# Weight sums from GpSimd to VectorE, half-piece reloads of token sums, and the final norm's weights, in a decoder layer on one core

## The chip, the cores and the metric

The kernel runs on one core of a Trainium2 chip. The metric is the time of one execution on the device in microseconds (us). The engines are TensorE (PE; its weight loads are PEld), VectorE (DVE), ScalarE (ACT), GpSimd (POOL) and SyncE (SP), which here only issues DMA transfers. Each engine takes its instructions strictly in the order of its own queue.

## The reference

One layer of a hybrid decoder, for 2048 tokens of width 1024 in float32: two kinds of attention side by side, then a feed-forward part with squared ReLU, then a norm. The part that matters here:

```python
h = h + jnp.einsum('bsm,md->bsd', mixed, w_out[l])
nm = rmsnorm(h, mlp_norm_g[l])
a = jnp.square(jax.nn.relu(jnp.einsum('bsd,df->bsf', nm, w_ff1[l])))   # 1024 -> 4096
h = h + jnp.einsum('bsf,fd->bsd', a, w_ff2[l])                         # 4096 -> 1024
return rmsnorm(h, final_norm_g)
```

## The kernel before

A float32 product is made as three matmuls of rounded parts: an operand is split into a high part (ScalarE copies with rounding) and a low part (VectorE subtracts), and `mm3` issues high × high, low × high and high × low. The products are also done by fast matrix schemes, which need fewer block products but sums of blocks beforehand.

**First feed-forward product.** The tokens are cut in two halves of 1024; each half is worked as 7 block products for each of 16 groups of columns, so 2 × 16 × 7 = 224 jobs (`jobs1`), each of 12 matmuls (`product1`). The seven sums of token blocks that a half needs were written to memory earlier (`hTD`), and are read back into a buffer `rb` and split into `TF` (tiles named `hb`) before the half's first job. There are two `rb` buffers of 128 × 2048. `reload(j, half)` starts the load of a whole sum, 1024 KB, and returns a generator whose two steps split half of it each. From job `first` = 105 on, where the last group of the first half begins, `parts_at` spreads the 14 half splits over the jobs 106 to 116; the second half's first job is 112. While `product1` runs, `act_sums` makes sums of the activations and writes them to `actD`.

**Second feed-forward product.** It is worked as 26 phases (`PRODUCTS`), each one block product of activations (`ca`, from `actD` by way of `ra`) and weights (`cb`). A phase has four steps, one for each quarter of the inner dimension; a step has 2 × 4 × 3 = 24 matmuls. The weights' operand of a step lies in one of four quarters of a state (`bs`), and the next phase's is made from it: where the table says `=`, `update_b` loads the state anew; where it says `+` or `-`, it adds a block that `fetch_b` has loaded into one of four buffers `rb` (in the profile these have the same name as the token buffers). `prep_b` then splits the state into one of three buffers `cb`, `prep_a` an activation block into one of three `ca`. In `update_b` the first sum of a step goes to GpSimd and a second one to VectorE (`engines=(G, V)`); only the four steps before the stage starts have both on VectorE. 88 sums are made: 22 of the table's entries, four steps each.

A new load of a state may start when VectorE has split the old one; a sum on it follows the load. `taken` adds a phase's result from PSUM to the running sums `acc2`, and where an output block is complete, `output` makes the final norm: two squares with a row sum on ScalarE, the factor `r`, one half of the row multiplied by `r` and the norm's weights on VectorE (line 1520), the other by the weights on GpSimd (1517) and by `r` on ScalarE (1521).

**Order.** The program is written as one sequence, and `tc` is made with `schedule_with_timeline_sim=True`: when the program is built, a planner runs it on a model of the engines and fixes each engine's queue in the order in which the instructions become ready there. So an instruction can stand in a queue ahead of others that were written before it.

```python
            update_b(n + 4)
            if n + 6 not in fetched:
                fetch_b(n + 6)
            prep_a(n + 2)
            prep_b(n + 2)
```

Of the kernel before, what the change touches and what calls it, by code (L numbers as in the profile page):

```python
# [13 lines left out]
AF = mybir.ActivationFunctionType  # L14
OP = mybir.AluOpType
# [101 lines left out]
def emit(tc, a, stop=99):  # L117
    nc = tc.nc
    V, A, G, T, SP = nc.vector, nc.scalar, nc.gpsimd, nc.tensor, nc.sync
# [6 lines left out]
    def ps(tag):  # L126
        return psum.tile([128, 512], F32, name="ps_" + tag, tag=tag, bufs=BANKS[tag])

    def slot(name, dt=F32, n=SLOT):

        return up.tile([128, SLOT], dt, name=name, tag="u", bufs=25)[:, :n]
# [34 lines left out]
    def stat(n=1):  # L166
        if stat_at[0] + n > 48:
            stat_at[0] = 0
        s = stats[:, stat_at[0]:stat_at[0] + n]
        stat_at[0] += n  # L170
        return s

    def rstd_of(ssq, width, n=1, bias=eps):
        r = stat(n)
        A.activation(r, ssq, AF.Ln, bias=bias, scale=1.0 / width)
        A.activation(r, r, AF.Exp, scale=-0.5)
        return r
# [46 lines left out]
    hTD = dram.tile([2, 7, 128, 4, 512], F32, name="hTD")  # L224
# [15 lines left out]
    CX, c11, c12, c21, c22, last = [t[:, GP * q:GP * q + GP] for t in acc for q in range(2)]  # L240
# [11 lines left out]
    order = (1, 2, 5, 6, 3, 4, 7)  # L252
# [4 lines left out]
    TF = {j: [slot(f"tb{j}", FR) for _ in range(2 if j < 7 else 1)] for j in order}  # L257
# [227 lines left out]
    def split(hi, lo, src):  # L485
        A.activation(hi, src, AF.Copy)  # L486
        V.tensor_tensor(lo, src, hi.bitcast(F32), op=OP.subtract)  # L487
# [109 lines left out]
    def reload(n):  # L597

        j, cs = order[n // 2], slice(1024 * (n % 2), 1024 * (n % 2) + 1024)
        t = (xp, bp)[n // 2 % 2][:, cs]  # L600
        SP.dma_start(t, nTD[j - 1].rearrange("p c s -> p (c s)")[:, cs])

        def rest():
            hi, lo = [v[:, cs] for v in TF[j]]
            tc.keep_in_program_order(A.activation(hi, t, AF.Copy))
            V.tensor_tensor(lo, t, hi.bitcast(F32), op=OP.subtract)
            if n + 4 < 14:
                back.append(reload(n + 4))

        return rest  # L610
# [121 lines left out]
    for at in range(7, len(jobs)):  # L732
        g = jobs[at][0]
# [419 lines left out]
    for pr in range(4):  # L1153
# [3 lines left out]
        for hh, br in seq:  # L1157
# [3 lines left out]
            first = len(units)  # L1161
# [62 lines left out]
    rb, TF, TB = [slot("rb")], {}, {}  # L1224
# [53 lines left out]
    order = (1, 2, 6, 5, 7, 3, 4)  # L1278
# [10 lines left out]
    def prep1(at):  # L1289

        if at >= len(jobs1):
            return
        g, j = jobs1[at]
        if not combs1:
            combs1.extend(view(c[:, 1024 * q:], (2, 4, 128)) for c in [slot("w1comb", FR) for _ in range(2)]
                          for q in range(2))
        r = raw1[g % 2]
        (a11, a12), (a21, a22) = [[r[:, 4 * k:4 * k + 4, n * 128:n * 128 + 128] for k in range(2)] for n in range(2)]
        c = combs1[at % 4]
        split(c[:, 0], c[:, 1], {1: a11, 2: a12, 6: a11, 5: a21, 7: a11, 3: a12, 4: a22}[j])  # L1300
        if j == 1:
            V.tensor_tensor(a21, a21, a22, op=OP.add)
            V.tensor_tensor(a11, a21, a11, op=OP.subtract)
        if j == 2:
            V.tensor_tensor(a12, a12, a11, op=OP.subtract)
        if j == 6:
            V.tensor_tensor(a11, a22, a11, op=OP.subtract)
        if j == 4:
            load_w1(g + 2)
# [80 lines left out]
    def some_sums(n=3):  # L1390

        for _ in range(n):
            while sums1 and next(sums1[0], 0) == 0:
                sums1.pop(0)
# [5 lines left out]
    for at, t in enumerate(tiles):  # L1400
# [8 lines left out]
        p = [ps("a"), ps("a")]  # L1409
        parts_ = 2 if at < 2 else 1  # L1410
        for q in range(parts_):
            for n in range(2):
                cs = slice(n * 512, n * 512 + 512)
# [20 lines left out]
    raw_a, comb_a, raw_b, comb_b, state, fin = [], [], [], [], [], {}  # L1434
# [5 lines left out]
    def load_a(n):  # L1440

        if n < 2 * NPH:
            p, k = divmod(n, 2)
            if len(raw_a) < 2:
                raw_a.append(view(slot("ra"), (4, 512)))
            SP.dma_start(raw_a[n % 2], actD[AT[p], :, 4 * k:4 * k + 4].rearrange("p q h s -> p q (h s)"))

    def prep_a(n):

        if n >= LAST:  # L1450
            return
        if len(comb_a) < 3:
            comb_a.append(view(slot("ca", FR), (2, 2, 512)))
        c, r = comb_a[n % 3], raw_a[n // 2 % 2][:, n % 2 * 2:n % 2 * 2 + 2]
        if PRODUCTS[n // 4][0] > 0:
            split(c[:, 0], c[:, 1], r)
        else:
            A.activation(c[:, 0], r, AF.Copy, scale=-1.0)
            V.scalar_tensor_tensor(c[:, 1], r, -1.0, c[:, 0].bitcast(F32), op0=OP.mult, op1=OP.subtract)
        if n % 2:  # L1460
            load_a(n // 2 + 2)
# [3 lines left out]
    def w2_part(n, k, m):  # L1465

        first = 8 * (n % 4) + 2 * (k % 2) + k // 2
        return w2[:, first:first + 5:4, 512 * m:512 * m + 512]

    def state_of(n):  # L1470

        if len(state) < 2:
            state.extend(view(slot("bs"), (4, 512)) for _ in range(2))
        return state[n % 4 // 2][:, n % 2 * 2:n % 2 * 2 + 2]

    def fetch_b(n):

        if n >= LAST:
            return
        if not raw_b:  # L1480
            raw_b.extend(view(v[:, 1024 * e:], (2, 512)) for v in [slot("rb2") for _ in range(2)] for e in range(2))
        fetched[n] = []
        for op, k, m in PRODUCTS[n // 4][2]:
            if op != "=":
                v = raw_b[turns[0] % 4]
                turns[0] += 1
                SP.dma_start(v, w2_part(n, k, m))
                fetched[n].append((op, v))

    def update_b(n, engines=(G, V)):  # L1490

        if n >= LAST:
            return
        v = state_of(n)
        for op, k, m in PRODUCTS[n // 4][2]:
            if op == "=":
                SP.dma_start(v, w2_part(n, k, m))
        for e, (op, r) in enumerate(fetched.pop(n)):
            engines[e].tensor_tensor(v, v, r, op=OP.add if op == "+" else OP.subtract)  # L1499

    def prep_b(n):

        if n >= LAST:
            return
        if len(comb_b) < 3:
            comb_b.append(view(slot("cb", FR), (2, 2, 512)))
        v = comb_b[n % 3]
        split(v[:, 0], v[:, 1], state_of(n))

    def output(C, row, i, last=False):  # L1510

        scr = fin["scr"][:, 512 * (i % 2):512 * (i % 2) + 512]
        ss, part = stat(2), stat()
        for n in range(2):
            A.activation(scr, C[n], AF.Square, accum_out=ss[:, n:n + 1])
            if n == 0:
                G.tensor_tensor(C[0], C[0], fin["g"][:, :512], op=OP.mult)
                A.activation(part, ss[:, 0:1], AF.Copy, bias=EPS, scale=1.0 / D)
        r = rstd_of(ss[:, 1:2], D, bias=part)
        V.scalar_tensor_tensor(C[1], C[1], r, fin["g"][:, 512:], op0=OP.mult, op1=OP.mult)  # L1520
        A.activation(C[0], C[0], AF.Copy, scale=r)
        SP.dma_start(out2[row:row + 128, 512:], C[1])
        (A if last else SP).dma_start(out2[row:row + 128, :512], C[0])

# [58 lines left out]

    first, parts_at = 7 * (NP - 1), {}
    for n in range(14):
        parts_at.setdefault(first + 1 + n * 4 // 5, []).append(n // 2)
    halves, begun = {}, set()
    for at in range(7, len(jobs1)):
        if at == first - 2:
            halves.update({n: reload(order[n], 1) for n in range(2)})  # L1590
        prep1(at + 2)
        some_sums()
        product1(at)
        for n in parts_at.get(at, ()):
            next(halves[n])
            if n in begun and n + 2 < 7:
                halves[n + 2] = reload(order[n + 2], 1)
            begun.add(n)
        n = at + 6 - len(jobs1)
        if n == 0:  # L1600
            load_a(0)
        if 0 <= n < 4:
            fetch_b(n)
            update_b(n, (V, V))
        if n == 3:
            load_a(1)
        if n in (3, 5):
            prep_b(n // 2 - 1)
            prep_a(n // 2 - 1)
            fetch_b(n // 2 + 3)  # L1610
# [4 lines left out]
    for ph, (_, chained, _, _) in enumerate(PRODUCTS):  # L1615
# [3 lines left out]
        for k in range(4):  # L1619
            n = 4 * ph + k  # L1620
# [74 lines left out]
```

## Time and profile before

| | us |
|---|---|
| median of 3 runs | 2280.32 (2277.76 to 2281.45) |
| the profiled execution | 2283.21 |
| its span, from the first to the last instruction | 2281.4 |
| PE busy | 2249.2 |
| VectorE busy | 1630.4 |
| ScalarE busy | 1230.4 |
| GpSimd busy | 544.3 |

In a row of the profile stand the line of the program, the engine, the operation, the tiles written and read, the shapes, the count, the busy time with the mean of one instruction in ns, and the idle time of the engine before these instructions with what ended it. A matmul counts as busy until its modelled end, so two neighbours overlap; how fast TensorE goes is seen from the starts. The granted clock is the share of TensorE's full speed. An "SPq" row is the issue of a transfer by SP; the transfer lands some us later.

### The profile page before, as it was taken

How to read it: one execution, taken by the hardware profiler on the slowest of the kernel's cores; microseconds unless marked ns; L12 is line 12 of the kernel's file. 1: busy time of each engine (PE TensorE's matmuls, PEld its weight loads, DVE VectorE, ACT ScalarE, POOL GpSimd, SP SyncE). 2: the span in 40 equal slices, each digit the busy share in tenths (PEclk: the TensorE clock that was granted, in tenths of full speed). 3: DMA queues.
4: the chain of work that ended last, by engine and by line, in shares of the span. 5: the costliest groups of instructions: out<-in, count | busy, mean ns of one | idle time of the engine just before them, and what ended most of it. 6: DMA issues, size and time to landing. Idle time of an engine off the chain costs nothing.

```text
span 2281.4 us, 35136 instructions
## 1 busy us (share of the span) xinstructions
PE 2249.2 (99%) x12508; PEld 1945.9 (85%) x12508; DVE 1630.4 (71%) x3065; ACT 1230.4 (54%) x2436; POOL 544.3 (24%) x482
## 2 busy tenths in 40 slices
PE   9999999999999999999999999999999999999998
PEld 8978998899999998888888887888888878888876
DVE  8788878766667676446777778777777577576778
ACT  6665436426877874234555556555555433333446
POOL 1210002024385672000000000000007562032465
PEclk9999999999999999999999999999999999999999
DMA  5458754776768864678544456555479988676775
GB/s 201 134 182 245 252 155 136 223 234 221 223 196 255 262 207 139 221 232 273 185 138 153 137 161 202 163 165 163 128 266 285 311 279 277 214 254 227 261 255 175
DMA packets 359920, 478.59 MB, mean 210 GB/s; under 512 B 19333, under 2 KB 268694, under 8 KB 347712
## 3 DMA queue, kind: packets, MB, share of 16 engines
q1 hardware_dynamic: 355246, 467.69, 63.6%
q0 software_dynamic: 4352, 8.39, 2.0%
q8 instruction: 98, 1.61, 0.3%
q14 instruction: 78, 0.64, 0.1%
q10 hardware_dynamic: 146, 0.27, 0.0%
HBM read 326.54 MB, written 154.44 MB: 211 GB/s over the span
## 4 chain that ended last, share of the span: by engine, by line
PE 84%; DMA 5%; POOL 3%; DVE 3%; issue 3%; ACT 2%; SPq 0%; POOLq 0%; ACTq 0%; DVEq 0%
PE ps_a L143 9%; PE ps_a L142 9%; PE ps_a L144 9%; PE ps_c L143 7%; PE ps_c L142 7%; PE ps_c L144 7%; PE ps_a L893 4%; PE ps_o L142 3%; PE ps_o L144 3%; PE ps_o L143 3%; PE ps_d L143 3%; PE ps_d L142 3%; PE ps_d L144 3%; PE ps_d L874 3%; PE ps_c L852 2%
## 5 line engine op out<-in xcount | busy, mean ns | idle before, releaser
L1499 POOL TENSOR_TENSOR bs<-bs,rb 128x1024 f32<-128x1024 f32 x72 | 217.7, 3031 | 1072.3 <-DMA actD<-ring 836.9
L486 ACT ACTIVATE cb<-bs 128x1024 fp32r<-128x1024 f32 x104 | 110.2, 1060 | 272.7 <-issue 116.2
L487 DVE TENSOR_TENSOR cb<-bs,cb 128x1024 fp32r<-128x1024 f32 x104 | 165.2, 1589 | 124.4 <-ACT cb L486 123.7
L487 DVE TENSOR_TENSOR w1comb<-w1raw,w1comb 128x512 fp32r<-128x512 f32 x224 | 153.8, 689 | 96.4 <-ACT w1comb L486 95.5
L486 ACT ACTIVATE w1comb<-w1raw 128x512 fp32r<-128x512 f32 x224 | 140.3, 628 | 81.6 <-PE ps_c L144 29.5
L865 ACT ACTIVATE pe<-pe,O 128x256 f32<-128x256 f32 (+1 forms) x384 | 156.5, 453 | 45.8 <-DVE O L864 42.3
L893 PE MATMUL ps_a<-v,pt 128*128 128x65 f32 x1200 | 178.5, 253 | 2.5 <-ACT pt L881 1.9
L893 PEld LDWEIGHTS ps_a<-v,pt 128*128 128x128 f32 x1200 | 175.4, 196 | 3.5 <-ACT pt L881 2.1
L874 PE MATMUL ps_d<-ident,pe 128*128 128x128 f32 x600 | 159.7, 279 | 0.0
L864 DVE CUSTOM_DVE_ANT_0 pe<-ps_c,nb 128x256 f32<-128x256 f32 (+1 forms) x384 | 126.3, 361 | 40.9 <-PE ps_d L874 18.3
L286 ACT ACTIVATE wcomb<-wraw 128x512 fp32r<-128x512 f32 (+2 forms) x119 | 90.0, 757 | 98.8 <-PE ps_a L143 34.5
L142 PE MATMUL ps_c<-hb,w1comb 128*128 128x512 f32 x336 | 131.0, 390 | 0.5 <-ACT xs L1371 0.5
L143 PE MATMUL ps_c<-hb,w1comb 128*128 128x512 f32 x336 | 130.9, 390 | 0.0
L144 PE MATMUL ps_c<-hb,w1comb 128*128 128x512 f32 x336 | 130.2, 390 | 0.0
L487 DVE TENSOR_TENSOR ca<-ra,ca 128x1024 fp32r<-128x1024 f32 x84 | 126.8, 1511 | 3.8 <-ACT ca L486 3.8
L142 PE MATMUL ps_c<-cb,ca 128*128 128x512 f32 x312 | 122.1, 391 | 0.0
L143 PE MATMUL ps_c<-cb,ca 128*128 128x512 f32 x312 | 122.0, 391 | 0.0
L144 PE MATMUL ps_c<-cb,ca 128*128 128x512 f32 x312 | 122.0, 391 | 0.0
L351 POOL TENSOR_TENSOR acc<-acc,misc 128x264 f32<-128x264 f32 (+1 forms) x32 | 38.7, 1221 | 313.1 <-DMA wraw<-w_in 200.3
L874 PEld LDWEIGHTS ps_d<-ident,pe 128*128 128x128 f32 x600 | 110.0, 187 | 0.1
L142 PE MATMUL ps_a<-wo,mT 128*128 128x512 f32 x256 | 101.4, 396 | 0.0
L1362 ACT ACTIVATE acc<-acc 128x512 f32<-128x512 f32 x96 | 60.7, 632 | 74.1 <-DVE acc L1381 44.0
(410 smaller groups left out, 7146.7 us busy)
## 6 DMA issues: line engine op xcount, KB each, us to landing
ra<-actD SPq DMA_DIRECT2D x52, 1024.0 KB, 7.3
actD<-ring SPq DMA_DIRECT2D x176, 256.0 KB, 2.5
rb<-w_ff SPq DMA_DIRECT2D x88, 512.0 KB, 6.1
bs<-w_ff SPq DMA_DIRECT2D x72, 512.0 KB, 6.1
w1raw<-w_ff SPq DMA_DIRECT2D x32, 1024.0 KB, 5.7
k<-kD SPq DMA_DIRECT2D x16, 1024.0 KB, 7.4
rb<-hTD SPq DMA_DIRECT2D x13, 1024.0 KB, 5.9
wraw<-w_in SPq DMA_DIRECT2D x48, 256.0 KB, 3.9
```

The costliest lines, as they stand in the source:

```text
L142: T.matmul(out, sh, mh, start=first, stop=False, **kw)
L143: T.matmul(out, sl, mh, start=False, stop=False, **kw)
L144: T.matmul(out, sh, ml, start=False, stop=last, **kw)
L286: A.activation(hi, src, AF.Copy, scale=sc)
L486: A.activation(hi, src, AF.Copy)
L487: V.tensor_tensor(lo, src, hi.bitcast(F32), op=OP.subtract)
L864: V.tensor_tensor_reduce(p, s, bias, scale=1.0, scalar=BIG, op0=OP.add, op1=OP.min, accum_out=nm)
L865: A.activation(p, p, AF.Exp, bias=nm, scale=-1.0)
L874: T.transpose(pb[:, i * 128:i * 128 + 128], src, ident)
L893: T.matmul(self.b.opsum[:, n % 4], self.pt[:, i * 128:i * 128 + 128], self.b.v[:, blk, cols], start=first, stop=last)
L1362: A.activation(v, v, AF.Relu)
L1499: engines[e].tensor_tensor(v, v, r, op=OP.add if op == "+" else OP.subtract)
```

## The change

Three edits. The sums of `update_b` are all made on VectorE. In `output`, the half that GpSimd and ScalarE worked on is multiplied by `r` and the weights in one instruction on VectorE, except for the very last output, which stays as it was. And the token sums of the second half are loaded in 14 pieces of 512 KB: four half buffers hold a piece each, the first four loads are issued at job 102 in place of two whole loads at job 103, and the load of piece n + 4 is issued behind the split of piece n. The jobs at which the pieces are split stay the same.

```diff
-    def update_b(n, engines=(G, V)):
+    def update_b(n, engines=(V, V)):
...
         for n in range(2):
             A.activation(scr, C[n], AF.Square, accum_out=ss[:, n:n + 1])
             if n == 0:
-                G.tensor_tensor(C[0], C[0], fin["g"][:, :512], op=OP.mult)
+                if last:
+                    G.tensor_tensor(C[0], C[0], fin["g"][:, :512], op=OP.mult)
                 A.activation(part, ss[:, 0:1], AF.Copy, bias=EPS, scale=1.0 / D)
         r = rstd_of(ss[:, 1:2], D, bias=part)
         V.scalar_tensor_tensor(C[1], C[1], r, fin["g"][:, 512:], op0=OP.mult, op1=OP.mult)
-        A.activation(C[0], C[0], AF.Copy, scale=r)
+        if last:
+            A.activation(C[0], C[0], AF.Copy, scale=r)
+        else:
+            V.scalar_tensor_tensor(C[0], C[0], r, fin["g"][:, :512], op0=OP.mult, op1=OP.mult)
...
     for n in range(14):
-        parts_at.setdefault(first + 1 + n * 4 // 5, []).append(n // 2)
-    halves, begun = {}, set()
+        parts_at.setdefault(first + 1 + n * 4 // 5, []).append(n)
+    piece = lambda n: rb[n // 2 % 2][:, 1024 * (n % 2):1024 * (n % 2) + 1024]
+
+    def load_piece(n):
+
+        if n < 14:
+            SP.dma_start(piece(n), hTD[1, order[n // 2] - 1][:, 2 * (n % 2):2 * (n % 2) + 2].rearrange("p c s -> p (c s)"))
+
     for at in range(7, len(jobs1)):
-        if at == first - 2:
-            halves.update({n: reload(order[n], 1) for n in range(2)})
+        if at == first - 3:
+            for n in range(4):
+                load_piece(n)
         prep1(at + 2)
         some_sums()
         product1(at)
         for n in parts_at.get(at, ()):
-            next(halves[n])
-            if n in begun and n + 2 < 7:
-                halves[n + 2] = reload(order[n + 2], 1)
-            begun.add(n)
+            cs = slice(1024 * (n % 2), 1024 * (n % 2) + 1024)
+            split(*[v[:, cs] for v in TF[order[n // 2]]], piece(n))
+            load_piece(n + 4)
```

## The prediction

> **What bounds the kernel now.** I read the page's engine rows first, then busy time by stretches, then the groups of matmuls with idle time.
>
> ```profile
> PE 2249.2 (99%) x12508; PEld 1945.9 (85%) x12508; DVE 1630.4 (71%) x3065; ACT 1230.4 (54%) x2436; POOL 544.3 (24%) x482
> ```
>
> The next rows are stretches: length, busy time of PE, PEld, DVE, ACT and POOL, granted clock, DMA share, GB/s.
>
> ```profile
> 1357.00:1402.00 45.00, 39.73 (x160) 31.89 (x159) 38.39 (x60) 31.59 (x49) 0.00 (x0) 0.92 0.63 205
> 1825.00:1875.00 50.00, 47.93 (x203) 37.06 (x202) 36.59 (x34) 16.63 (x17) 29.75 (x12) 1.00 0.89 282
> 1875.00:2160.00 285.00, 285.00 (x1259) 236.11 (x1258) 193.45 (x171) 107.77 (x116) 79.69 (x32) 1.00 0.75 250
> 2160.00:2190.00 30.00, 25.74 (x102) 20.73 (x101) 29.35 (x18) 15.45 (x31) 26.88 (x11) 0.89 0.73 249
> 2190.00:2262.00 72.00, 70.53 (x311) 58.08 (x310) 59.29 (x47) 38.96 (x83) 44.38 (x18) 1.00 0.58 192
> ```
>
> PE is the bound, and where it is undisturbed it runs without a hole: 285 us for 1259 matmuls is 0.2264 us each, so one step of the second product (24 matmuls) takes 5.43 us. All that the change can give back are the holes. Around the switch of token halves 45.00 − 39.73 = 5.3 us are idle, and the clock of 0.92 costs another 0.08 × 45 = 3.6: 8.9 together. In the second product 2.1, then 4.3 with 0.11 × 30 = 3.3 for the clock, then 1.5: 11.2. That makes 20.1 us in all.
>
> ```profile
> L142 PE MATMUL ps_d<-hb,w1comb 128*128 128x512 f32 x4 | 2.2, 556 | 2.7 <-ACT xs L1371 2.7
> L143 PE MATMUL ps_a<-cb,ca 128*128 128x512 f32 x2 | 1.4, 713 | 4.3 <-DVE ca L487 4.3
> L143 PE MATMUL ps_a<-cb,ca 128*128 128x512 f32 x1 | 0.5, 505 | 1.5 <-DVE ca L487 1.5
> ```
>
> These are PE's groups at 1370, 2176 and 2249 us: after waits of 2.7 and 4.3 us the matmuls last 556 and 713 ns on average (half clock for a while), after 1.5 us there is no such tail.
>
> **Half pieces at the switch.** PE waited there for ScalarE's copy out of PSUM, and ScalarE stood behind a split whose load had not landed:
>
> ```profile
> 1370.36 1.06 ACT L486 ACTIVATE hb<-rb 128x1024 fp32r<-128x1024 f32 x1 [1.66 <-DMA rb<-hTD]
> 1371.33 0.61 ACT L1363 ACTIVATE acc<-acc 128x512 f32<-128x512 f32 x1
> 1393.40 2.00 ACT L486 ACTIVATE hb<-rb 128x1024 fp32r<-128x1024 f32 x2 [2.86 <-DMA rb<-hTD]
> ```
>
> From issue to landing those 1024 KB loads took (shortest, median, longest):
>
> ```profile
> DMA to landing us min/median/max: 4.9/5.9/8.5
> ```
>
> The change issues 14 loads of 512 KB instead of 7 of 1024 KB, the first four one job earlier, each later one right behind the split that frees its half. The spacing from a piece's load to its use becomes four pieces, so both waits (1.66 and 2.86) should go. Seven more issues on SP cost 0.33 each and stand in front of stores that nobody waits for closely. A half load's own time is not shown: the 512 KB loads of weights (row further down: 4.0 shortest, 6.1 median) bound it; I take 5, as half the bytes should not take longer than 5.9. A piece is split every 0.8 jobs of 12 matmuls, 2.2 us, so four pieces leave 8.7 us. ScalarE is dense here, so I keep a small wait: a gain of 7.5, between 3 and 8.9.
>
> [...]
>
> **Final norm on VectorE.**
>
> ```profile
> L1520 DVE SCALAR_TENSOR_TENSOR sum<-sum,stats,gf x16: 739/1770/2895, 2163.0 to 2276.0; 128x512 f32<-128x512 f32 x16
> L1521 ACT ACTIVATE sum<-sum,stats x16: 706/711/726, 2167.0 to 2276.1; 128x512 f32<-128x512 f32 x16
> ```
>
> 15 products on POOL and 15 scalings on ScalarE (0.71 each) go; 15 more multiplies come to VectorE. Its existing twin takes from 0.74 to 2.9 us; the long ones lie beside POOL's products, which go, so I take 0.74. In the tail the three scalings before the last one leave ScalarE's queue: about 1 us gained, 0 to 2. On VectorE 4 × 0.74 = 3.0 us are added per phase that outputs.
>
> **Sums on VectorE: the direct cost.**
>
> ```profile
> L487 DVE TENSOR_TENSOR cb<-bs,cb x104: 1208/1226/3598, 1682.3 to 2262.5; 128x1024 fp32r<-128x1024 f32 x104
> L1499 POOL TENSOR_TENSOR bs<-bs,rb x72: 2386/3296/5019, 1715.7 to 2243.3; 128x1024 f32<-128x1024 f32 x72
> L1499 DVE TENSOR_TENSOR bs<-bs,rb x16: 1215/1226/1227, 1670.6 to 1867.7; 128x1024 f32<-128x1024 f32 x16
> DMA to landing us min/median/max: 4.0/6.1/10.8
> ```
>
> 72 sums of 3.3 us on POOL become 72 of 1.23 on VectorE (1.14 from start to start). VectorE's splits, now up to 3.6 us when POOL holds them up, fall back to 1.2. VectorE has room: 193 of 285 us.
>
> **Sums on VectorE: the new wait.** A sum adds to a state that in 18 of 26 phases is first loaded anew ("="). That load starts when VectorE's split of the old state ends. Ten phases besides the first have "=" and a sum: 40 steps. On POOL the wait for the load held up nobody. On VectorE whatever is queued behind it stands, and what that is the trace tells. SP:
>
> ```profile
> 2066.09 0.37 SPq L1487 DMA_DIRECT2D rb<-w_ff  x1
> 2066.55 0.42 SPq L1497 DMA_DIRECT2D bs<-w_ff  x1
> 2070.70 0.37 SPq L1497 DMA_DIRECT2D bs<-w_ff  x1
> 2074.72 0.37 SPq L1487 DMA_DIRECT2D rb<-w_ff  x1
> 2075.80 0.37 SPq L1497 DMA_DIRECT2D bs<-w_ff  x1
> ```
> POOL and VectorE beside it:
> ```profile
> 2063.38 2.68 POOL L1499 TENSOR_TENSOR bs<-bs,rb 128x1024 f32<-128x1024 f32 x1 [20.12 <-DMA bs<-w_ff]
> 2072.28 2.41 POOL L1499 TENSOR_TENSOR bs<-bs,rb 128x1024 f32<-128x1024 f32 x1 [6.22 <-DMA bs<-w_ff]
> 2076.11 3.06 POOL L1499 TENSOR_TENSOR bs<-bs,rb 128x1024 f32<-128x1024 f32 x1 [1.42 <-DMA bs<-w_ff]
> 2080.69 2.95 POOL L1499 TENSOR_TENSOR bs<-bs,rb 128x1024 f32<-128x1024 f32 x1 [1.52 <-DMA bs<-w_ff]
> ```
> ```profile
> 2067.07 0.67 DVE L1556 TENSOR_TENSOR sum<-sum,ps_a 128x512 f32<-128x512 f32 x1
> 2069.46 1.21 DVE L487 TENSOR_TENSOR cb<-bs,cb 128x1024 fp32r<-128x1024 f32 x1
> ```
>
> The refill `rb` at 2066.09 needs POOL's sum of one step to be over, and it stands ahead of the next step's `bs` load, which needs only the next split. So the planner that fixed the order believed: load and sum are over before the next split is. With a sum half as long it will believe so all the more, and on VectorE it will put the sum ahead of the next split. Where VectorE has sums today, the order is that already:
>
> ```profile
> 1837.96 1.23 DVE L1499 TENSOR_TENSOR bs<-bs,rb 128x1024 f32<-128x1024 f32 x1 [2.29 <-POOL bs L1499]
> 1839.10 1.22 DVE L487 TENSOR_TENSOR cb<-bs,cb 128x1024 fp32r<-128x1024 f32 x1
> 1843.75 1.23 DVE L1499 TENSOR_TENSOR bs<-bs,rb 128x1024 f32<-128x1024 f32 x1 [2.29 <-POOL bs L1499]
> 1844.89 1.22 DVE L487 TENSOR_TENSOR cb<-bs,cb 128x1024 fp32r<-128x1024 f32 x1
> ```
>
> There a split every 1844.89 − 1839.10 = 5.79 us against PE's 5.43 makes the idle 2.1 us of 1825 to 1875. That loop (split, POOL's sum, VectorE's sum) gets shorter. But 40 other steps get a loop of their own: split (2070.70 − 2069.46 = 1.24 to the issue), load to sum (2072.28 − 2066.55 = 5.73, 5.41, 4.89: mean 5.3), sum 1.14: 7.7 us, 2.25 over PE's step.
>
> What PE can lend is what the triple buffers hold:
>
> ```profile
> 2099.57 1.06 ACT L486 ACTIVATE cb<-bs 128x1024 fp32r<-128x1024 f32 x1 [3.38 <-PE ps_c L143]
> 2101.81 1.22 DVE L487 TENSOR_TENSOR ca<-ra,ca 128x1024 fp32r<-128x1024 f32 x1
> ```
>
> PE frees a buffer at 2099.55, the operand is ready at 2103.03, and it is needed two steps later: 10.86 − 3.46 = 7.4 us of slack. The sums of the last one load the steps in runs: five of 4 steps, one of 8, one of 12, with lighter phases between that win the slack back. Over the slack: 5 × (9.0 − 7.4) + (18.0 − 7.4) + (27.0 − 7.4) = 8.0 + 10.6 + 19.6 = 38. Partial sums out of PSUM (0.60 from start to start, four or eight at a phase's end) are partly queued behind the blocked sum too; half of them, 22 in all these phases, add 13. So +51, while the old 11.2 us of holes vanish.
>
> **Sum.** 51 − 11.2 − 7.5 − 1 = +31 us. The profiled execution took 2283.2 (span 2281.4 and 1.8 around it), the median shown is 2280.3, which I add to: 2311. Unknown is above all the load's time. At 4.0 the loop is 6.4, the 12-step run alone exceeds the slack by some 4 and half the partial sums count: about −8 net. At 6.1 it is 8.5: 25 + 17 + 29 + 13, and 6 for the multiplies of the norm, is 90, net +70.
>
> **Rivals.** *The sums land behind the next split* (chance 0.18): then no load is waited for, every hole closes, and the time is 2280.3 − 20.1 − 1 = 2259 with the tail. For it: VectorE's free time, and a thin margin: if the planner prices POOL's sum at its shortest (2.39), it starts by 5.43 − 2.39 = 3.0 us after a split, and the next split starts 5.43 − 1.22 = 4.2 after it, so 1.2 us more in the planner's load would turn the order. Against it: the refill's place on SP, the same at each step of these rows. [...]
>
> *The loop exists but the loads get faster* (0.09): with loads at 4.0 to 4.4, gains and stalls cancel within 10 us: about 2275.
>
> *It is worse* (0.08): loads near the median of 6.1, VectorE late with the norm as well: 2350.
>
> *Half loads don't come sooner* (inside all cases): 512 KB may take 6.1; the switch then keeps its 8.9 and the forecast is 7.5 more.
>
> **Numbers.** Forecast 0.65, from 2285 to 2345 by itself; the range for all goes down to 2259, as the first rival has to be half inside. Faster or slower count from 0.2% (4.6 us, about what a measurement can tell): faster 0.20, same 0.06, slower 0.74.
>
> **What would show it.** Right: VectorE's sum rows wait for `bs` loads 2 to 4 us each, splits 7 to 8 us apart in those phases, PE's idle time behind VectorE from 2000 us on, no wait for `hTD` above 1 us. Wrong: sums without waits, or splits ahead of them, with PE whole through the second product.

## The result and the profile after

The changed kernel takes 2283.94 us (median of 22 runs, 2278.61 to 2287.07); the kernel before took 2280.12 beside it (22 runs, 2275.51 to 2283.78). The ratio is 1.0013, with a 95% interval of 1.0007 to 1.0019: 0.13% slower, 3 to 4 us, where 31 were forecast. Engine rows of the page, and the stretches that the prediction read:

```profile
PE 2247.9 (98%) x12508; PEld 1941.5 (85%) x12508; DVE 1638.1 (72%) x3152; ACT 1221.5 (54%) x2421; POOL 304.9 (13%) x395
```
```profile
1090.00:1110.00 20.00, 17.41 (x68) 13.56 (x68) 11.90 (x22) 9.14 (x17) 0.00 (x0) 0.91 0.64 200
1357.00:1402.00 45.00, 42.83 (x185) 33.96 (x184) 40.72 (x65) 33.97 (x52) 0.00 (x0) 1.00 0.66 219
1825.00:1875.00 50.00, 50.00 (x222) 41.38 (x221) 48.12 (x49) 18.32 (x18) 4.85 (x4) 1.00 0.93 312
1875.00:2160.00 285.00, 276.29 (x1201) 225.62 (x1200) 178.04 (x178) 100.84 (x100) 2.41 (x2) 0.99 0.72 232
2160.00:2190.00 30.00, 27.29 (x119) 21.76 (x119) 24.78 (x30) 16.76 (x38) 0.00 (x0) 1.00 0.80 275
2190.00:2262.00 72.00, 72.00 (x319) 59.64 (x318) 65.19 (x73) 38.65 (x81) 0.00 (x0) 1.00 0.69 230
```

The old holes have closed or shrunk: the half switch is idle 2.2 us instead of 5.3 and at full clock, 1825 to 1875 is whole, so is the end. New holes have opened: 285.00 − 276.29 = 8.7 us where PE was whole before, and a place that the prediction did not look at, 1090 to 1110 us, in the first product.

The forecast's wait is there. VectorE's group of the sums, and the landing of the states' loads (shortest, median, longest):

```profile
L1499 DVE TENSOR_TENSOR bs<-bs,rb 128x1024 f32<-128x1024 f32 x88 | 107.5, 1222 | 101.2 <-DMA bs<-w_ff 96.5 <-DMA rb<-w_ff 4.4
```
```profile
DMA to landing us min/median/max: 4.0/5.2/12.9
```

VectorE stands 96.5 us before sums whose state has not landed. In some phases it is step for step the loop that was forecast (VectorE in order of time):

```profile
2063.38 1.23 DVE L1499 TENSOR_TENSOR bs<-bs,rb 128x1024 f32<-128x1024 f32 x1 [3.43 <-DMA bs<-w_ff]
2064.52 1.22 DVE L487 TENSOR_TENSOR cb<-bs,cb 128x1024 fp32r<-128x1024 f32 x1
...
2071.17 1.22 DVE L1499 TENSOR_TENSOR bs<-bs,rb 128x1024 f32<-128x1024 f32 x1 [2.50 <-DMA bs<-w_ff]
2072.31 0.68 DVE L1560 TENSOR_TENSOR sum<-sum,ps_c 128x512 f32<-128x512 f32 x1
2072.91 1.22 DVE L487 TENSOR_TENSOR cb<-bs,cb 128x1024 fp32r<-128x1024 f32 x1
...
2079.20 1.23 DVE L1499 TENSOR_TENSOR bs<-bs,rb 128x1024 f32<-128x1024 f32 x1 [3.94 <-DMA bs<-w_ff]
2080.34 1.22 DVE L487 TENSOR_TENSOR cb<-bs,cb 128x1024 fp32r<-128x1024 f32 x1
```

Splits come 8.39 and 7.43 us apart (7.7 forecast; PE's step is 5.43). In others they come in pairs:

```profile
2136.16 1.22 DVE L487 TENSOR_TENSOR cb<-bs,cb 128x1024 fp32r<-128x1024 f32 x1
...
2138.43 1.22 DVE L487 TENSOR_TENSOR cb<-bs,cb 128x1024 fp32r<-128x1024 f32 x1
2142.42 1.23 DVE L1499 TENSOR_TENSOR bs<-bs,rb 128x1024 f32<-128x1024 f32 x1 [2.78 <-DMA bs<-w_ff]
...
2146.49 1.22 DVE L1499 TENSOR_TENSOR bs<-bs,rb 128x1024 f32<-128x1024 f32 x1
2147.63 0.68 DVE L1560 TENSOR_TENSOR sum<-sum,ps_o 128x512 f32<-128x512 f32 x1
2148.23 1.22 DVE L487 TENSOR_TENSOR cb<-bs,cb 128x1024 fp32r<-128x1024 f32 x1
```

Two splits free two states, two loads run side by side, VectorE waits once: 2148.23 − 2136.16 = 12.1 us for two steps, with four partial sums in it. Counted through the 40 steps by VectorE's order in the trace, 26 sums stand directly behind the split that frees their state, and 14 have one more split between; in the phases that follow such a phase without a break (16, 21, 22) at least every other one.

The hole in the first product is another queue of the same kind. VectorE before, then after:

```profile
1094.24 0.69 DVE L1307 TENSOR_TENSOR w1raw<-w1raw 128x512 f32<-128x512 f32 x1
1096.53 0.69 DVE L1302 TENSOR_TENSOR w1raw<-w1raw 128x512 f32<-128x512 f32 x1 [1.60 <-DMA w1raw<-w_ff]
```
```profile
1099.44 0.69 DVE L1302 TENSOR_TENSOR w1raw<-w1raw 128x512 f32<-128x512 f32 x1 [3.43 <-DMA w1raw<-w_ff]
1100.05 0.68 DVE L1307 TENSOR_TENSOR w1raw<-w1raw 128x512 f32<-128x512 f32 x1
```

L1302 belongs to the next group of weights, L1307 to the present one, whose operand PE needs. They have changed places, so L1307 stands behind a load that it has no use for. And the load comes later. SP before, then after:

```profile
1080.94 0.32 SPq L1251 DMA_DIRECT2D rb<-hTD  x1
...
1087.01 0.32 SPq L1251 DMA_DIRECT2D rb<-hTD  x1
1087.61 0.38 SPq L1287 DMA_DIRECT2D w1raw<-w_ff  x1
```
```profile
1082.75 5.25 SPq L1596 DMA_DIRECT2D rb<-hTD  x3
...
1089.34 0.49 SPq L1596 DMA_DIRECT2D rb<-hTD  x1
1089.92 0.82 SPq L1287 DMA_DIRECT2D w1raw<-w_ff  x1
```

The planner had already moved the first two whole loads, written for job 103, some 280 us ahead of their use, to 1080.94 and 1087.01 us; the change makes four issues of these two at the same place. The load of the weights stands right behind the last of them in both kernels. It is issued at 1089.92, before at 1087.61; as the kernel after had come 1.6 us later to this place, 0.7 us of that are new. Why the planner then let L1302 and L1307 change places, no trace shows.

From one profiled execution to the other, PE is 3.5 us further behind after the hole at 1099 us, gains 5.5 at the half switch, takes 590.4 us instead of 587.4 from the second product's first matmul to its last, and is 1.2 quicker behind it. That is −0.2; the profiled spans differ by 1.4, since 1.6 was there already at 1090 us. So this pair does not show the +3.8 of the medians: the profiled execution of the kernel before was 3.1 us over its median, that of the kernel after 0.7. What each part of the change costs is settled by the runs below.

### The profile page after: what moved, and what is told of

It is laid out like the page before. It is cut to its first block, busy times and chain, and to the rows that moved or that the text cites. A ratio compares the mean times of both kernels' runs of the same rounds, so it can differ in the third digit from the quotient of the medians.

```text
span 2282.8 us, 35105 instructions
## 1 busy us (share of the span) xinstructions
PE 2247.9 (98%) x12508; PEld 1941.5 (85%) x12508; DVE 1638.1 (72%) x3152; ACT 1221.5 (54%) x2421; POOL 304.9 (13%) x395
## 3 DMA queue, kind: packets, MB, share of 16 engines
q0 software_dynamic: 4352, 8.39, 2.0%
## 4 chain that ended last, share of the span: by engine, by line
PE 68%; issue 23%; DMA 3%; DVE 2%; POOL 2%; ACT 1%; SPq 0%; POOLq 0%; DVEq 0%; ACTq 0%
PE ps_a L142 8%; PE ps_a L143 8%; PE ps_a L144 8%; PE ps_c L142 5%; PE ps_c L143 5%; PE ps_c L144 5%; PE ps_a L893 4%; PE ps_o L144 3%; PE ps_o L142 3%; PE ps_o L143 3%; PE ps_d L874 3%; PE ps_d L143 2%; PE ps_d L142 2%; PE ps_d L144 2%; PE ps_c L852 2%
## 5 line engine op out<-in xcount | busy, mean ns | idle before, releaser
L1499 DVE TENSOR_TENSOR bs<-bs,rb 128x1024 f32<-128x1024 f32 x88 | 107.5, 1222 | 101.2 <-DMA bs<-w_ff 96.5
L487 DVE TENSOR_TENSOR cb<-bs,cb 128x1024 fp32r<-128x1024 f32 x104 | 126.9, 1220 | 54.8 <-ACT cb L486 54.4
L1548 POOL DMA_DIRECT2D sum<-hD x16 | 19.5, 1277 | 1057.9 <-ACT sum L1557 859.9
L487 DVE TENSOR_TENSOR ca<-ra,ca 128x1024 fp32r<-128x1024 f32 x84 | 102.3, 1219 | 0.1
```

## The experiments

Each is compared with the kernel before, run beside it on the same chip (2280.1 to 2280.6 us).

**The parts alone.** First the half pieces alone (e1); the norm alone (e2); the sums alone (e3); and half pieces and norm together (e4). The diffs are shortened.

```diff
 e1:  -def update_b(n, engines=(V, V)):
      +def update_b(n, engines=(G, V)):      # and the norm as before
 e2:  only output() of the change
 e3:  only engines=(V, V)
 e4:  the whole change with engines=(G, V)
```

> The kernel before with the half-piece loads alone. Theory A (the half pieces do two things: they close most of the holes at the half switch, 9.0 us lost there before and 3.4 after, and they pull VectorE's sum of the next weights, L1302, in front of L1307 at 1099 us, where PE then lost about 3.5 us more than before): -5.5 + 3.5 = -2, about 2278, with the hole at 1099 us in the trace. Rival B (the hole at 1099 us is chance or belongs to another part): -5.5, about 2274.5, no hole there. The forecast's own term: -7.5, about 2272.5.

> The kernel before with only the final norm's products moved to VectorE. Theory A: the tail gives 1.2, and with POOL's products gone VectorE's long operations near 2176 us (up to 3.6) get short, so the hole there (4.3 us and the half clock behind it, 7.6 in all) is partly closed: -3, about 2277 (2273 to 2279). Rival B: that hole is made by POOL's sums, not its products, and stays: -1, about 2279. The forecast's term for this part alone: -1.

> The kernel before with only the second product's sums all on VectorE. Theory A (the waits for reloaded states are there, but the order puts the sum ahead of the next split in only part of the 40 steps, so little more than the triple buffers' slack is used up): second product +3 to +7 net of the old holes, about 2285 (2282 to 2288). The forecast's working (sum ahead in all 40 steps): +51 - 11.2, about 2320. Rival C (the waits cost nothing and the old holes go): -11, about 2269.

> The whole change without the sums on VectorE (they stay on GpSimd and VectorE as before). Theory A: the parts add up, -2 - 3 = -5, about 2275 (2273 to 2278), so the sums on VectorE cost about 9 us of the kernel after. Rival C (the sums cost nothing or gain): no faster than the kernel after, about 2284.

| | us, median | ratio to before, 95% interval |
|---|---|---|
| half pieces | 2279.34 | 0.9994 (0.9985 to 1.0003) |
| norm | 2276.99 | 0.9987 (0.9978 to 0.9995) |
| sums | 2288.49 | 1.0035 (1.0023 to 1.0046) |
| half pieces and norm | 2275.59 | 0.9976 (0.9967 to 0.9985) |

All four came out as theory A had it, −1.3, −3.7, +7.9 and −5.0; only the sums alone lie half a us above its range. For the norm the interval (2275.6 to 2279.5) still holds rival B's 2279; there PE's waits decide, shown in the section on why the prediction was wrong. The parts add up to +2.9, the whole is +3.8; and the sums cost 2283.94 − 2275.59 = 8.4 us of the kernel after. The hole at 1099 us is there in the kernels with half pieces (the first row, 1090 to 1110 us with half pieces alone) and not without them (second row, sums alone):

```profile
1090.00:1110.00 20.00, 17.45 (x69) 13.63 (x68) 11.82 (x22) 8.53 (x16) 0.00 (x0) 0.91 0.69 207
```
```profile
1090.00:1110.00 20.00, 19.54 (x86) 15.59 (x85) 14.32 (x25) 10.96 (x19) 0.00 (x0) 1.00 0.70 223
```

So rival B on the half pieces is out: they give at the switch and take most of it back 260 us earlier.

**The order of the sums.** Two kernels add to the kernel after an edge that fixes which instruction of VectorE comes first, and move the calls so that it can be set (shortened).

```diff
 e5, sum n behind split n-2 (and called behind it):
+            if e == 0 and n - 2 in lows: add_manual_dep(sum n, lows[n - 2], NoSync)
 e6, sum n ahead of split n-3 (called one step earlier):
+        if n + 3 in sums: add_manual_dep(low part of split n, sums[n + 3], NoSync)
```

> The kernel after, with each sum on VectorE held behind the split of two steps before its use (the load of a state then has two steps, 10.9 us, until its sum has its turn). Theory A (what the second product still loses, 16.3 us of PE time in the kernel after, comes from sums that stand on VectorE ahead of the next split and wait there for their load): nearly all of it goes, -13, about 2271 (2266 to 2276), splits evenly 5.4 us apart. Rival D (the losses come from VectorE's own amount of work and from the loads' bandwidth, whatever the order): no faster than 2281.

> The kernel after, with each sum on VectorE held ahead of the split three steps before its use, in every step: the order that the forecast took for granted. Theory A (the forecast's working of the loop was right, only the order was in part another): the forecast's sum comes out, 2284 - 16 + 51 = 2319 (2305 to 2335), splits 7.5 to 8 us apart in all phases with reloaded states and a sum. Rival E (the working was wrong too: the wait per step or the share that reaches PE is much smaller than reckoned): 2284 to 2294.

Measured, with the ratio to before and its interval: **2267.49 us** with the sums behind (0.994, 0.9926 to 0.9953), **2314.83** with the sums ahead (1.0154, 1.0141 to 1.0168). Sums behind, the sums' group and the stretch from 1875 to 2160 us:

```profile
L1499 DVE TENSOR_TENSOR bs<-bs,rb 128x1024 f32<-128x1024 f32 x88 | 107.3, 1219 | 9.7 <-DMA rb<-w_ff 5.8 <-DMA bs<-w_ff 4.0
```
```profile
1875.00:2160.00 285.00, 285.00 (x1259) 235.96 (x1259) 193.15 (x196) 112.08 (x134) 2.41 (x2) 1.00 0.76 250
```

The same 88 sums, as long as before, wait 4.0 us for states instead of 96.5, and PE has no hole. Rival D is out: VectorE's amount of work costs PE nothing. The moved calls do not bring the loads forward: in the kernel after and in both of these, a state's load is issued 0.03 us (median) after the split that frees it. Sums ahead, VectorE's waits from 1700 to 2262 us (total, times, longest), and the stretches of the run of 8 steps and the run of 12:

```profile
DVE bs L1501 <- DMA bs<-w_ff: 123.3, 35, 8.2
```
```profile
2031.00:2064.00 33.00, 27.37 (x110) 21.17 (x109) 19.67 (x20) 10.14 (x10) 0.00 (x0) 0.95 0.60 200
2145.00:2222.00 77.00, 61.10 (x245) 47.28 (x244) 55.04 (x59) 26.63 (x48) 0.00 (x0) 0.93 0.73 245
```

Idle 5.6 and 15.9 us, with the clock's 0.05 × 33 and 0.07 × 77 it is 7.3 and 21.3; the forecast had 10.6 and 19.6, without its share of partial sums. 39 of the 40 sums stand directly behind the split that frees their state. This is the kernel that the prediction worked out, and its time is 2315 against the 2311 forecast. Rival E is out.

**How many steps the loop spans.** The same edge, one step earlier (e5b).

```diff
-            if e == 0 and n - 2 in lows:
+            if e == 0 and n - 3 in lows:
```

> As the kernel with sums held behind the split of two steps before their use, but held behind the split of three steps before: one step earlier, so that one more split stands between the split that frees a state and the sum, where the forecast's loop had none. Theory A (the loop of 7.7 us, 1.24 + 5.3 + 1.14, now spans two of PE's steps, 10.9 us, so it stays shorter than PE): about 2268 (2264 to 2271), no PE loss, though VectorE waits about 1 us for loads in many steps. Rival G (any wait of VectorE for a load reaches PE in part): 2272 to 2278.

Measured 2268.47 (0.9945, 0.9933 to 0.9958), as theory A said; VectorE's waits in the second product:

```profile
DVE bs L1499 <- DMA bs<-w_ff: 18.7, 15, 6.2
```

VectorE waits 18.7 us and PE not at all in the second product. One split more in the loop is enough; rival G is out.

**The sums alone, in order.** The kernel before with all sums on VectorE and the edge of e5 (e10).

> The kernel before with all sums on VectorE, held behind the split of two steps before their use; no half pieces, no norm. Theory A (sums on VectorE are a gain once their order is right: the second product's old losses of 13.3 us all go, the holes at the half switch stay): about 2268.5 (2266 to 2272), against 2288.5 for the same sums in the order they got by themselves. Rival H (the gain of the ordered kernels needs the norm's products off GpSimd as well): 2274 to 2280.

Measured 2268.65 (0.9947, 0.9935 to 0.996), 19.8 us under the same sums without the edge. The holes at the half switch are still there, 4.5 us idle (first row), the long stretch of the second product is whole (second row):

```profile
1357.00:1402.00 45.00, 40.55 (x171) 32.70 (x170) 39.85 (x62) 33.29 (x51) 0.00 (x0) 0.96 0.66 214
1875.00:2160.00 285.00, 285.00 (x1259) 236.00 (x1258) 193.78 (x192) 113.36 (x134) 10.41 (x6) 1.00 0.76 248
```

Rival H is out. With all sums on VectorE the kernel gains 11.9 us in the right order and loses 7.9 in the one the planner made: here the place in the queue decided, not the engine's speed. The shortest sum on GpSimd takes 2386 ns against a median of 1226 on VectorE; GpSimd's median of 3296 is 2.7 times as long.

**The hole at 1099 us.** L1302 is held behind L1307: in the kernel after (e7), in that with ordered sums (e8), and in that without the sums (e9).

```diff
+            if g: add_manual_dep(L1302, the last L1307, NoSync)
```

> The kernel after, with VectorE's sum of the next group's weights (L1302) held behind the last combination of the group before (L1307) in the first product. Theory A (PE's stall at 1099 us comes from L1302 standing in front of L1307 and waiting for its load): the stall goes, -3.5, about 2280.5, if nothing else moves. Rival F (the stall comes from the later landing of the weights on a busier queue, whatever VectorE's order): 2284.

> The kernel after with both edges: sums behind the split of two steps before their use, and L1302 behind L1307. Theory A: the two gains add up, -13 - 3.5, about 2267.5 (2263 to 2273), faster than both kernels. If D and F hold: 2284.

> Half pieces and norm with the sums as before, and L1302 held behind L1307 in the first product. Theory A (the half pieces cost 3.9 us at 1099 us by that order, and nothing else moves): -3 on the 2275.6 of the same kernel without the edge, about 2272.5. Rival F2 (the edge closes that stall but what it delays costs as much elsewhere, as the kernel after with the edge, at 2284.2, leaves open): 2275.6.

Measured: 2284.22 (1.0019, 1.0008 to 1.003), **2265.83** (0.9939, 0.9927 to 0.9951) and 2275.03 (0.9972, 0.996 to 0.9984). Beside the same kernels without the edge that is +0.3, −1.7 and −0.6. The hole itself closes; PE's wait there falls from 2.1 us to 0.6 in the kernel after with the edge:

```profile
PE ps_d L143 <- DVE w1comb L487: 0.6, 1, 0.6
```

So theory A is right on the cause of the stall, though the kernel's time is the one that rival F gave: on the way from 1092 to 1232 us, PE gains 3.2 us (kernel after) and 3.1 (no sums). But the gain doesn't arrive at the end. Without the sums, 1.2 us of it goes again at the half switch and 2.4 in the second product; in the kernel after, the profiled execution was 3.1 us late before the place began and lost 2.0 in the second product. Whether the edge causes any of this, as rival F2 has it, or whether it is the scatter of single executions, stays open: all three differences lie within the intervals, and so would the 3 us that e9 was to gain.

The version with both edges, 2265.83, has the lowest median, 0.6% under the kernel before and 0.8% under the one after; its lead over e5 (2267.49) lies within the intervals.

## Why the prediction was wrong

**The step that failed** is in the new wait: "on VectorE it will put the sum ahead of the next split", taken for all 40 steps. It was so in 26. The row that carried it, SP's refill at 2066.09, comes from phase 18, one of the three in which all four sums stand so; the prediction found it "the same at each step of these rows" and held that for all phases. In the long runs, from which 10.6 + 19.6 of the 38 us came, seven of the 12 steps of the later phases have a second split in the loop. There the splits come in pairs: in the run of 12 the second splits of three pairs start at 2138.43, 2150.50 and 2160.25 us, 21.8 us for four steps (22.9 in the run of 8), against the 21.7 that PE takes for four. So little more of the slack is used up. How far PE falls behind the kernel with the sums behind, by the starts of the phases' first matmuls:

| us | run of 8 | run of 12 | five runs of 4 | second product |
|---|---|---|---|---|
| forecast | 10.6 | 19.6 | 8.0 | 51, with 13 for partial sums in all runs |
| sums ahead (e6) | 8.5 | 20.8 | 19.2 | 48.5 |
| kernel after | 3.5 | 7.8 | 5.4 | 16.7 |

The term was +51; the runs showed 2288.49 − 2268.65 = 19.8 us as the price of the order that the planner made, and 2314.83 − 2267.49 = 47.3 as that of the order assumed.

**What held in the same term.** The load (5.3 taken, median 5.2), the loop (7.7; splits 8.4 and 7.4 apart), the slack, PE's loss for the runs of 8 and 12 steps, and the size of the term: e6 tests them all at once, 48.5 against 51. That its time comes within 4 us of the forecast is in part luck: the runs of 4 cost more than reckoned and the run of 8 less, and the other terms were reckoned at −19.7 where e5 gained 12.6. The first rival's mechanism is e10 and e5: its 2259 was 8 us too low against e5. The half switch kept 2.9 us of idle time there, and the hole at 1099 us, 1.6 us of waiting in that kernel, was not foreseen; and the 20.1 us of holes were read in an execution 2.9 us longer than the median from which they were subtracted.

**The old holes in the second product, −11.2.** Right with ordered sums: between the medians of e10 and before lie 11.9.

**The half pieces, −7.5.** At the switch right in kind: idle and clock together are 8.9 before and 2.2 after. But this profile of before lost more there than others with the old loads, where it is 6.1 to 6.6 (norm alone, sums alone, and e10, whose row of 45 us stands above), so the gain is some 4 us, not 6.7. Waits for `hTD` were to stay under 1 us; three a little longer are left (ScalarE):

```profile
1375.17 1.06 ACT L486 ACTIVATE hb<-rb 128x1024 fp32r<-128x1024 f32 x1 [1.05 <-DMA rb<-hTD]
...
1379.00 1.06 ACT L486 ACTIVATE hb<-rb 128x1024 fp32r<-128x1024 f32 x1 [1.25 <-DMA rb<-hTD]
...
1388.54 1.06 ACT L486 ACTIVATE hb<-rb 128x1024 fp32r<-128x1024 f32 x1 [1.05 <-DMA rb<-hTD]
```

What was missed is that the first loads are issued 280 us early, in another stretch, as they were before the change, and that VectorE's order changes there with the half pieces. "Stand in front of stores that nobody waits for closely" looked at the wrong stretch: the load behind them was that of the next weights. The hole there costs 3.5 us. Net −1.3 (interval −3.4 to +0.7) instead of −7.5.

**The norm, −1.** Mis-sized: −3.7 alone (interval −1.1 to −5.0). The prediction had counted both old holes after 2160 us, at 2176 and 2249, to the sums; with the norm's products off GpSimd the second is gone and the first is smaller. PE's waits from 2165 to 2262 us (total, times, longest) before, with half pieces alone, and with the norm alone:

```profile
PE ps_a L143 <- DVE ca L487: 5.7, 2, 4.3
```
```profile
PE ps_a L143 <- DVE ca L487: 4.7, 2, 3.2
```
```profile
PE ps_a L143 <- DVE ca L487: 2.6, 1, 2.6
```

The other two profiles with the new norm and the old sums (e4 and e9) have one wait each too, of 2.9 and 3.0 us. The 15 added multiplies last 0.745 us at the median in the kernel after (0.74 taken). The tail's 1 us is not settled: 1.2 in the kernel after, but 0.7 or 0.8 also in profiles with the old norm.

## What to carry to other kernels

The same 88 sums, at 1.22 us each, gave 2314.83 us ahead (e6) and 2267.49 behind (e5): here the price of work on another engine was set less by its duration than by what stood behind it in that engine's queue while it waited for a load. When work moves, reckon the loop from freeing a buffer to its next use, divide by the number of consumer steps it spans, and compare that with the consumer's step. One more step in the loop turned +35 us (e6) into −12 (e5b) here. Where a planner fixes the order, read it at every step and not at one phase, and look also at how far ahead it pulls loads: a change to them shows there, not where they are used.

## What the runs showed of the hardware

The length of a wait alone did not settle whether the clock halved. From 1080 us on, the granted clock was 0.50 for 3.41 us behind PE's waits of 2.6 and 2.7 us in the kernel before, for 6.82 us behind its wait of 4.3, and for 3.41 us behind each of the two waits of 2.1 in the kernel after. It stayed at 1.00 behind the wait of 1.5 us before (2249 us) and behind that of 1.8 after (2175 us). The two waits of 2.1 us, each in a stretch of 3.41 us with the next one:

```profile
1098.46:1101.87 3.41, 1.28 (x6) 0.77 (x5) 2.43 (x5) 1.10 (x2) 0.00 (x0) 1.00 0.85 259
1101.87:1105.28 3.41, 3.41 (x10) 2.68 (x9) 2.95 (x7) 1.05 (x3) 0.00 (x0) 0.51 0.47 156
2136.20:2139.61 3.41, 1.36 (x6) 0.86 (x5) 3.41 (x4) 2.02 (x2) 0.00 (x0) 1.00 0.70 223
2139.61:2143.02 3.41, 3.41 (x9) 2.63 (x8) 0.63 (x2) 0.00 (x0) 0.00 (x0) 0.50 0.92 294
```

In the kernel after, stretches of half clock begin at 863.0, 1101.9 and 2139.6 us, 70 and 304 times 3.413 us apart; counted from the first instruction they lie 2.9 us past a whole number of these, and 1.7 in the kernel before. The fastest version has a wait of 2.6 us at 1389 us, and its clock stays whole (1.00):

```profile
1387.69:1391.10 3.41, 1.76 (x8) 1.13 (x6) 3.41 (x8) 3.41 (x7) 0.00 (x0) 1.00 0.28 96
1391.10:1394.51 3.41, 2.43 (x11) 2.02 (x12) 3.41 (x7) 3.13 (x6) 0.00 (x0) 1.00 0.30 101
1394.51:1397.92 3.41, 2.95 (x13) 2.18 (x12) 3.41 (x7) 1.12 (x2) 0.00 (x0) 1.00 0.22 73
```

PE's idle time is 1.65 us in the first row here and 0.98 in the second (3.41 − 1.76, 3.41 − 2.43), where each wait of 2.1 us left 2.1 in one row. Why the clock halved behind those and not behind this one, no run shows. A stretch at half clock costs 0.50 × 3.41 = 1.7 us, an estimate from these rows; so a wait of 2.1 us may cost nearly twice as much where one follows it as where none does.
